# A hybrid attention layer on one core: the first two left factors of the last products loaded once, under the scans

## The chip, the cores and the metric

The kernel runs on one core of one Trainium2 chip. The metric is the time of one execution on the device in microseconds (us). Five engines work in parallel, each through its own list of instructions in order: TensorE (PE; its weight loads are listed as PEld), VectorE (DVE), ScalarE (ACT), GpSimd (POOL) and SyncE (SP). SP and POOL also start the transfers (DMA) between the core's memory and the device's main memory.

## The reference

One encoder layer on 1024 tokens of width 1024, with 16 learned meta tokens in front of them. `_gla_chunked` and `_neighbourhood_attention` stand in the reference above this part.

```python
h = concatenate([meta_tokens, x])
u = _rmsnorm(h, norm_g)
z = u @ w_in
gq, gk, gv, r_f, r_b, g_gate, nq, nk, nv, n_gate = split(z)
q, k, v = gq * GLA_DK ** -0.5, gk, gv                      # 4 heads of 128 keys, 256 values
lg_f = log_sigmoid(r_f @ w_decay_fwd + b_decay_fwd) / 16   # rank 16
lg_b = log_sigmoid(r_b @ w_decay_bwd + b_decay_bwd) / 16
o_f = _gla_chunked(q, k, v, lg_f)                          # a scan over chunks, one per direction
o_b = flip(_gla_chunked(flip(q), flip(k), flip(v), flip(lg_b)))
o_gla = _rmsnorm(o_f + o_b, gla_out_norm_g) * silu(g_gate)
qn, kn = _rmsnorm(nq, q_norm_g), _rmsnorm(nk, k_norm_g)    # 16 heads of 64
o_na = _neighbourhood_attention(qn, kn, nv, rpb, meta_bias) * silu(n_gate)
out = (h + concatenate([o_gla, o_na]) @ w_out)[16:]
```

The last line's product has an inner dimension of 2048: 1024 of `o_gla` and 1024 of `o_na`.

## The kernel before, in words

**Numbers in two parts.** A float32 factor is split into a high part (ScalarE copies it into a shorter format: `wh`, `uh`, `oh`, `lf[0]`, `kn[0]`) and a low part (VectorE subtracts the high part from the number: `wl`, `ul`, `ol`, `lf[1]`, `kn[1]`). `mm3` (L409) makes one product from three matmuls: high by high (L411), high by low (L412) and low by high (L413).

**Stages.** First the neighbourhood attention, eight pairs of heads `p`, with the input projection's matmuls as filler between its small matmuls. Then the gated linear attention of four heads `h` (`gla`, L1030): decays, a backward scan of seven steps (n = 7 to 1), a forward scan of eight (n = 0 to 7), again with projections as filler. Filler of the last head is the first part of the output projection: the rows of `w_out` for `o_na`, 16 steps `j` of two halves `f` (`out_proj`). At its end come the last products (`out_last`).

**The last products.** The rows of `w_out` that belong to `o_gla` make a product of two by two blocks, which is computed with seven block products in place of eight. `m` = 0 to 6 counts them, n = 0 to 3 the 128 columns within one, so there are 28 steps `j` = 4m + n of 12 matmuls. Their left factors are, in order, quadrant 11, quadrant 12, the sums s1, s4, s2, s3 and quadrant 22; `R` holds the quadrants (512 x 512, in four pieces of 256 KB) and the sums. Their right factors are blocks of `w_out` and the sums T and U, which accumulating transfers on POOL's queue build (L1426) and which are split like weights. `X` and `Y` are accumulators in TensorE's output memory; V takes -X after product 0.

**What sets the order.** `Sched` plans on a clock of its own, in TensorE's nanoseconds. `("gap", ns)` puts filler in for that long; `defer(ns, fn)` issues an operation when the clock has come that far; `PK_NS` is the gap ahead of a head's backward scan, `WD_NS` and `WD_LOW_NS` are deferrals of the decays' weights. What is fixed there is the order of each engine's list; on the chip each instruction waits for what it needs, and everything behind it on its engine waits too.

**Lines that the prediction names.** `wd_prep` (L1009) clears (POOL, L1012), copies (ScalarE, L1013) and completes (VectorE, L1016 and L1017) the decays' weights, at p = 2 for one direction and p = 4 for the other. L753 is VectorE's first step of a softmax, L772 and L774 its normalization, L792 VectorE's copy of transposed probabilities `PT`, L805 the matmuls that gather values with them. In a scan, L1161 transposes a chunk `pk` of the keys `ga` (made at L1107), L1163 and L1164 make its two parts `kn`, and `pu` are the matmuls on them; `at` and `ah` (L1244 to L1248) are VectorE's mask and parts of the chunk's scores, read by `po`. L262 and L263 make `wh` and `wl` of a projection's weight, L257 and L258 those of `w_out`, T and U. L1291 loads halves of 128 columns for the output projection (`oin`), L1308 and L1309 split them (`oh`), L1341 accumulates a half's result (`pout`) into `acc`. L1366 loads a piece of a quadrant (`r`), L1375 makes a sum's piece (`rs`, or into `r`), L1385 and L1389 split a left factor (`lf`), L1424 loads U, L1430 copies -X to V.

Buffers that matter: `oh` has three, `lf` five, weights nine (`NW`), each given back when TensorE has read it for the last time. The pool `op` is there from the last head on, the pool `tp` (quadrants, U) from the end of the scans on, in memory that the scans had.

Of the kernel before, what the change touches and what calls it, by code (L numbers as in the profile page):

```python
# [8 lines left out]
F32 = mybir.dt.float32  # L9
# [3 lines left out]
OP = mybir.AluOpType  # L13
# [24 lines left out]
PV_AT = (0.5, 0.5, 0.5, 0.6, 0.5, 0.5, 0.5, 0.5)  # L38
STEP_AT = (0.78, 2.0, 3.0, 4.0, 4.92, 6.0, 7.08, 8.0)
BWD_NS = (1800.0, 1523.0, 1844.0, 1892.0)  # L40
PK_NS = (3500.0, 2300.0, 2300.0, 2300.0)
AT_NS = 1085.0
R_NS = 2800.0
R0_NS = 1200.0
# [14 lines left out]
SILU_STEP = 1  # L59

WD_AT = (2, 4)
WD_NS = 20000.0
WD_LOW_NS = 5000.0

class Sched:

# [75 lines left out]
def kernel(  # L142
# [866 lines left out]
    def wd_prep(d):  # L1009

        st, w = G["wst"], G["wd"][d]
        pool.memset(f32(w[96:128]), 0.0)  # L1012
        act.activation(w[0:98], st[0:98], AF.Copy)  # L1013

        def low():
            dve.tensor_tensor(w[64:96], st[64:96], f32(w[64:96]), OP.subtract)  # L1016
            dve.scalar_tensor_tensor(w[96:98], f32(w[96:98]), ident[96:98, 97:98], st[96:98], OP.mult, OP.subtract)  # L1017

        S.defer(WD_LOW_NS, low)

    def decay_static():

# [251 lines left out]


    acc, oh, ol, op = {}, {}, {}, []
    steps = [(g, n) for g in (2, 3) for n in range(8)] + [(g, n) for g in (0, 1) for n in range(4)]
    R = {}

    def out_proj():  # L1280

        ld = {}

        def load(j):
            if j < len(steps):
# [12 lines left out]

        def halves(j):
            if j < len(steps):  # L1300
                g, n = steps[j]
                t = ld.pop(j)
                if j == 0:
                    o = shr.tile([128, 2, 4, 128], F32R, tag="zt", name=f"oh{g}_{n}", bufs=3)
                else:
                    o = op[0].tile([128, 2, 4, 128], F32R, tag="oh", name=f"oh{g}_{n}", bufs=3)
                oh[j], ol[j] = o[:, 0], o[:, 1]
                act.activation(oh[j], t, AF.Copy)  # L1308
                dve.tensor_tensor(ol[j], t, f32(oh[j]), OP.subtract)  # L1309

        def ahead(j):
            halves(j + 1)
            load(j + 3)

        for j in range(2):
            load(j)
        x_in(0)
        yield from dense_gg(3, lambda: halves(0))
        upool_cm.__exit__(None, None, None)
        op.append(ostack.enter_context(tc.tile_pool(name="op", bufs=1, side="right")))  # L1320
        load(2)
        for j in range(1, 4):
            x_in(j)
        for j, (g, n) in enumerate(steps[:16]):
            ahead(j)
            x_in(j + 4)
            if j == 9:
                wsum["T"] = op[0].tile([128, 4, 512], F32, name="T")
                sp.dma_start(wsum["T"], w_block(0, 0))
            if j == 11:  # L1330
                pool.dma_start(wsum["T"], w_block(0, 1), accum_op=OP.add)
            for f in range(2):
                ps = ps_tile("pd", f"pout{g}_{n}_{f}", 2)
                for k in range(4):
                    wh, wl = weights(("o", g), 4 * f + k)
                    mm3(ps, oh[j][:, k], ol[j][:, k], wh, wl, k == 0, k == 3)
                    if n == 7:
                        release()
                    yield 648
                a = acc[n][:, f * 512 : f * 512 + 512]  # L1340
                dve.tensor_tensor(a, a, ps, OP.add)  # L1341

        yield from out_last(ahead)

    def weights(key, i):
        while (key, i) not in split:
# [5 lines left out]

    def out_tiles(tp):

        for q in (22, 21, 11, 12, "s1", "s2"):
            R[q] = tp.tile([128, 4, 512], F32, name=f"r{q}")
        wsum["U"] = tp.tile([128, 4, 512], F32, name="U")
        op.append(tp)

    def rv(q, n):  # L1360
        return R[q][:, :, 128 * n : 128 * n + 128]
# [3 lines left out]
        ts = slice(512 * h + 128 * n, 512 * h + 128 * n + 128)  # L1365
        sp.dma_start(rv(q, n), o_scr[4 * g : 4 * g + 4, :, ts].rearrange("f p t -> p f t"))  # L1366

    def out_last(ahead):


        sums = {"s1": ("s1", 21, 22), "s2": ("s2", 11, "s1"), "s4": (12, 12, "s2"), "s3": (21, 21, 11)}
# [1 line left out]
        def add(s, n):  # L1373
            d, a, b = (rv(q, n) for q in sums[s])
            dve.tensor_tensor(d, a, b, OP.subtract)  # L1375

        left = (11, 12, "s1", 12, "s2", 21, 22)
        opnd = {}

        def operand(m, n):  # L1380

            t = rv(left[m], n)
            o = op[1].tile([128, 2, 4, 128], F32R, tag="lf", name=f"lf{m}_{n}", bufs=5)
            sign = -1.0 if m == 6 else 1.0
            act.activation(o[:, 0], t, AF.Copy, scale=sign)  # L1385
            if m == 6:
                dve.scalar_tensor_tensor(o[:, 1], t, -1.0, f32(o[:, 0]), OP.mult, OP.subtract)
            else:
                dve.tensor_tensor(o[:, 1], t, f32(o[:, 0]), OP.subtract)  # L1389
            opnd[m, n] = o  # L1390

        V = [op[0].tile([128, 512], F32, name=f"V{n}") for n in range(4)]

        def quad(q, n):
            return acc[n + 4 * (q // 10 - 1)][:, 512 * (q % 10 - 1) : 512 * (q % 10)]
# [13 lines left out]

        todo = {j: [] for j in range(28)}  # L1410
        for n in range(4):
            for q, j in ((22, (3, 3, 4, 4)), (21, (3, 3, 4, 4)), (11, (5, 5, 6, 6)), (12, (7, 7, 8, 8))):
                todo[j[n]].append(lambda q=q, n=n: quadrant_in(q, n))
            todo[5 + n].append(lambda n=n: add("s1", n))
            todo[7 + n].append(lambda n=n: add("s2", n))
            todo[9 + n].append(lambda n=n: add("s4", n))
            todo[15 + n].append(lambda n=n: add("s3", n))
            for m in range(2, 7):
                todo[4 * m + n - 2].append(lambda m=m, n=n: operand(m, n))
            todo[13 + n].append(lambda n=n: plus(11, n, X[n], store=True))  # L1420
            todo[18 + n].append(lambda n=n: [pool.dma_start(quad(q, n), V[n], accum_op=OP.add) for q in (12, 22)])
            todo[21 + n].append(lambda n=n: plus(21, n, V[n], OP.subtract))
            todo[21 + n].append(lambda n=n: put(12, n))
        todo[8].append(lambda: sp.dma_start(wsum["U"], w_block(1, 1)))  # L1424
        for j, (t, g, f) in {8: ("T", 1, 1), 10: ("U", 0, 1), 16: ("T", 1, 0)}.items():
            todo[j].insert(0, lambda t=t, g=g, f=f: pool.dma_start(wsum[t], w_block(g, f), accum_op=OP.add))  # L1426

        def result(m, n):
            if m == 0:
                act.activation(V[n], X[n], AF.Copy, scale=-1.0)  # L1430
            elif m == 2:
                plus(22, n, Y[n])
            elif m == 3:
                plus(12, n, Y[n])
# [6 lines left out]

        for j in range(28):
            m, n = divmod(j, 4)
            if j < 8:
                ahead(16 + j)
            for fn in todo[j]:
                fn()
            P = X if m in (0, 1, 4) else Y
# [3 lines left out]
            first = m in (0, 2, 4, 5)  # L1452
            for k in range(4):
                wh, wl = weights(("m", m), k)
                a, b = (oh[16 + j], ol[16 + j]) if m < 2 else (opnd[m, n][:, 0], opnd[m, n][:, 1])
                mm3(P[n], a[:, k], b[:, k], wh, wl, first and k == 0, k == 3, not first)
                if n == 3:
                    release(1000.0 * k)
                yield 648
# [147 lines left out]
```

## Time and profile before

| | us |
|---|---|
| median of three runs | 1122.23 |
| lowest and highest | 1119.29, 1124.56 |
| profiled execution, its own time | 1118.37 |
| its span | 1116.6 |
| TensorE busy | 1099.4 (98%) |
| VectorE busy | 750.4 (67%) |
| ScalarE busy | 564.5 (51%) |
| GpSimd busy | 220.7 (20%) |

The span is the profiled execution's from its first to its last instruction; its own time has 1.8 us more. The attention takes the span to about 600 us, the four heads' scans from there to about 1032, the last products from about 1028 to the end. The granted clock of TensorE was full in all but the last stretch. Rows of the timeline give start, duration and idle time of the engine before the row with what ended it; "x6" merges neighbours, and the end of a matmul is modelled, so matmuls overlap in the rows.

### The profile page before, as it was taken

What the parts mean: (1) busy time and instruction counts of PE and PEld (TensorE: products, weight loads), DVE (VectorE), ACT (ScalarE), POOL (GpSimd) and SP (SyncE); (2) the same over time, 40 slices, a digit from 0 to 9 for tenths busy, and PEclk for the clock granted to TensorE, in tenths of its full rate; (3) what the DMA queues carried; (4) which work ended last, traced back from release to release, by engine and by line L of the source; (5) the groups of instructions that cost most, each with busy time, mean ns of one, the idle gap of its engine ahead of it and who ended that gap; (6) DMA issues with size and microseconds to landing.
All of it is one profiled execution on the core that took longest, in us unless ns stands there. A gap on an engine that the chain in (4) does not pass through costs nothing.

```text
span 1116.6 us, 18945 instructions
## 1 busy us (share of the span) xinstructions
PE 1099.4 (98%) x6691; PEld 970.7 (87%) x6691; DVE 750.4 (67%) x1854; ACT 564.5 (51%) x1464; POOL 220.7 (20%) x442
## 2 busy tenths in 40 slices
PE   8999999999999999999999999999999999999998
PEld 7899898989989899898898789889889977887776
DVE  4666666776666767666764975776596578656485
ACT  6756475674656657565555441642443254313431
POOL 2733232332323233231100001000101000010011
PEclk9999999999999999999999999999999999999999
DMA  8720302112021210302124412503612365352967
GB/s 277 234 59 20 104 10 84 56 39 86 9 84 56 75 58 2 121 12 60 60 58 123 143 49 75 160 25 82 179 38 72 91 205 177 104 133 85 269 137 184
DMA packets 83591, 108.67 MB, mean 97 GB/s; under 512 B 6884, under 2 KB 51300, under 8 KB 83496
## 3 DMA queue, kind: packets, MB, share of 16 engines
q1 hardware_dynamic: 74344, 91.85, 26.5%
q0 software_dynamic: 8864, 15.47, 6.5%
q8 instruction: 53, 0.87, 0.3%
q14 instruction: 42, 0.34, 0.1%
q10 hardware_dynamic: 288, 0.14, 0.0%
HBM read 80.10 MB, written 21.04 MB: 91 GB/s over the span
## 4 chain that ended last, share of the span: by engine, by line
PE 83%; DVE 6%; ACT 3%; DMA 3%; SPq 2%; issue 1%; POOL 1%; DVEq 0%; POOLq 0%; ACTq 0%
PE pn_na L411 7%; PE pn_na L413 6%; PE pn_na L412 6%; PE po L805 4%; PE pp L786 3%; PE pn_gv L411 3%; PE pn_gv L413 3%; PE pn_gv L412 3%; PE pz_gz L411 3%; PE pz_na L413 3%; PE pz_na L412 3%; PE pz_na L411 3%; PE pz_gg L411 3%; PE pz_gz L412 3%; PE pz_gz L413 3%; PE pz_gg L412 3%
## 5 line engine op out<-in xcount | busy, mean ns | idle before, releaser
L411 PE MATMUL pn_na<-wh,uh 128*128 128x384 f32 x512 | 177.9, 347 | 2.0 <-ACT uh L362 1.2
L412 PE MATMUL pn_na<-wl,uh 128*128 128x384 f32 x512 | 172.7, 337 | 0.4 <-DVE wl L263 0.4
L413 PE MATMUL pn_na<-wh,ul 128*128 128x384 f32 x512 | 172.5, 337 | 0.2
L263 DVE SCALAR_TENSOR_TENSOR wl<-raw,gT,wh 128x256 fp32r<-128x256 f32 (+4 forms) x168 | 89.9, 574 | 37.6 <-ACT wh L262 36.7
L411 PEld LDWEIGHTS pn_na<-wh,uh 128*128 128x128 f32 x512 | 96.2, 188 | 8.0 <-issue 4.6
L262 ACT ACTIVATE wh<-raw,gT 128x256 fp32r<-128x256 f32 (+4 forms) x168 | 88.1, 576 | 21.9 <-PE pz_gz L412 14.0
L758 ACT ACTIVATE P<-P,sm 128x384 f32<-128x384 f32 x96 | 58.5, 609 | 77.9 <-DVE sm L753 77.2
L412 PEld LDWEIGHTS pn_na<-wl,uh 128*128 128x128 f32 x512 | 96.4, 188 | 1.7 <-DVE wl L263 1.3
L413 PEld LDWEIGHTS pn_na<-wh,ul 128*128 128x128 f32 x512 | 96.2, 188 | 0.9 <-DVE ul L364 0.9
L213 POOL TENSOR_SCALAR post<-post 128x1 f32<-128x1 f32 x32 | 6.9, 215 | 375.8 <-ACT on L1212 375.8
L214 POOL TENSOR_TENSOR ss<-ss,epsm 128x4 f32<-128x4 f32 x64 | 74.5, 1163 | 5.3
L411 PE MATMUL pn_gv<-wh,uh 128*128 128x256 f32 (+1 forms) x256 | 75.3, 294 | 0.0
L413 PE MATMUL pn_gv<-wh,ul 128*128 128x256 f32 (+1 forms) x256 | 72.8, 284 | 0.0
L412 PE MATMUL pn_gv<-wl,uh 128*128 128x256 f32 (+1 forms) x256 | 72.7, 284 | 0.0
L753 DVE CUSTOM_DVE_ANT_0 P<-s,wt 128x416 f32<-128x416 f32 (+1 forms) x128 | 65.4, 547 | 1.0
L774 DVE TENSOR_SCALAR P<-P,sm 128x384 f32<-128x384 f32 (+1 forms) x128 | 58.3, 455 | 11.5 <-ACT P L758 0.5
L1212 ACT ACTIVATE on<-po 128x256 f32<-128x256 f32 x32 | 12.3, 383 | 89.6 <-PE po L413 89.4
L772 DVE RECIPROCAL sm<-sm 128x1 f32<-128x1 f32 x128 | 20.8, 162 | 53.3 <-POOL sm L760 49.0
L411 PE MATMUL pz_na<-uh,wh 128*128 128x512 f32 x128 | 53.2, 416 | 0.0
L411 PE MATMUL pout<-wh,oh 128*128 128x512 f32 x128 | 52.3, 409 | 0.2 <-DVE acc L1341 0.2
L411 PE MATMUL pz_gz<-uh,wh 128*128 128x512 f32 x128 | 52.5, 410 | 0.0
L786 PE MATMUL pp<-ident,P 128*128 128x128 f32 (+1 forms) x384 | 52.5, 272 | 0.0
(378 smaller groups left out, 3030.1 us busy)
## 6 DMA issues: line engine op xcount, KB each, us to landing
raw<-in_w_na_dram SPq DMA_DIRECT2D x56, 256.0 KB, 3.4
v_scr<-gvst SPq DMA_DIRECT2D x64, 128.0 KB, 2.3
raw<-in_w_o_dram SPq DMA_DIRECT2D x28, 256.0 KB, 3.2
v<-v_scr POOLq DMA_DIRECT2D x4, 1536.0 KB, 9.1
oin<-o_scr SPq DMA_DIRECT2D x24, 256.0 KB, 3.3
VM<-vnat SPq DMA_DIRECT2D x8, 512.0 KB, 3.5
o_scr<-ng SPq DMA_DIRECT2D x8, 512.0 KB, 2.6
raw<-in_w_gz_dram SPq DMA_DIRECT2D x16, 256.0 KB, 2.7
```

The source lines that it names most:

```text
L214: pool.tensor_tensor(dst, dst, epsm[: dst.shape[0], :eng_n], OP.pow)
L262: act.activation(wh[:, ts], r[:, ts], AF.Copy, scale=g)
L263: dve.scalar_tensor_tensor(wl[:, ts], r[:, ts], g, f32(wh[:, ts]), OP.mult, OP.subtract)
L411: pe.matmul(ps, ah, bh, start=start, stop=False, skip_group_check=more)
L412: pe.matmul(ps, ah, bl, start=False, stop=False, skip_group_check=more)
L413: pe.matmul(ps, al, bh, start=False, stop=stop, skip_group_check=more)
L753: dve.tensor_tensor_reduce(P[:, :n], ps[:, :n], wt[2 * p + a][:, off : off + n], -1.0, 3.0e38, OP.add, OP.min, mx)
L758: act.activation(loc, loc, AF.Exp, scale=-1.0, bias=mx, accum_out=sm[:, a : a + 1])
L772: dve.reciprocal(r, s)
L774: dve.tensor_scalar(loc, loc, r, None, OP.mult)
L786: pe.transpose(pp[:w, c * 128 : c * 128 + 128], Ps[a][0][:, c0 : c0 + w], ident)
L805: pe.matmul(po[0][64 * a : 64 * a + 64, u4 * 128 : u4 * 128 + 128], V[:, 64 * a : 64 * a + 64], PT[a][:w, c * 128 : c * 128 + 128], start= ...
```

## The change

It has five parts. (1) Quadrants 11 and 12 are loaded once, in pieces, during steps 12 to 15 of the output projection, which run under the last head's scans; they are the left factors of products 0 and 1 and the quadrants of the later sums. Before, products 0 and 1 loaded the same numbers as eight more halves `oin`, and the quadrants were loaded after the scans. (2) The left factors of all products are split by `operand`, two steps ahead; the first two are split within the output projection's last two steps. The sums come one step earlier, and the accumulating transfers stand last in their steps and not first. (3) The copy of -X to V is issued at the start of steps 3 and 4 and not after each step of product 0, and V lies in the pool `tp`. (4) The decays' weights are cleared and copied earlier, and their two low parts are issued apart. (5) The gap ahead of the first head's backward scan is shorter, and the halves of step 1 of the output projection are split after the first half of step 0.

```diff
-PK_NS = (3500.0, 2300.0, 2300.0, 2300.0)
+PK_NS = (2900.0, 2300.0, 2300.0, 2300.0)
...
-WD_NS = 20000.0
-WD_LOW_NS = 5000.0
+WD_NS = 11000.0
+WD_LOW_NS = (7900.0, 20100.0)
...
         def low():
             dve.tensor_tensor(w[64:96], st[64:96], f32(w[64:96]), OP.subtract)
+
+        def low_bias():
             dve.scalar_tensor_tensor(w[96:98], f32(w[96:98]), ident[96:98, 97:98], st[96:98], OP.mult, OP.subtract)
 
-        S.defer(WD_LOW_NS, low)
+        S.defer(WD_LOW_NS[0], low)
+        S.defer(WD_LOW_NS[1], low_bias)
...
-    steps = [(g, n) for g in (2, 3) for n in range(8)] + [(g, n) for g in (0, 1) for n in range(4)]
+    steps = [(g, n) for g in (2, 3) for n in range(8)]
...
-        for j, (g, n) in enumerate(steps[:16]):
-            ahead(j)
+        for j, (g, n) in enumerate(steps):
+            if j:
+                halves(j + 1)
+            load(j + 3)
             x_in(j + 4)
...
             for f in range(2):
+                if (j, f) == (0, 1):
+                    halves(1)
...
+            if j == 10:
+                for q in (11, 12):
+                    R[q] = op[0].tile([128, 4, 512], F32, name=f"r{q}")
+            if j > 11:
+                quadrant_in(11, j - 12)
+                quadrant_in(12, j - 12)
+            if j > 13:
+                operand(0, j - 14)
+        yield from out_last()
...
-        for q in (22, 21, 11, 12, "s1", "s2"):
+        for q in (22, 21, "s1", "s2"):
             R[q] = tp.tile([128, 4, 512], F32, name=f"r{q}")
         wsum["U"] = tp.tile([128, 4, 512], F32, name="U")
         op.append(tp)
+        V.extend(tp.tile([128, 512], F32, name=f"V{n}") for n in range(4))
...
+    def operand(m, n):
+
+        t = rv(left[m], n)
+        if m < 2:
+            o = op[0].tile([128, 2, 4, 128], F32R, tag="oh", name=f"lf{m}_{n}", bufs=3)
+        else:
+            o = op[1].tile([128, 2, 4, 128], F32R, tag="lf", name=f"lf{m}_{n}", bufs=5)
...
-            for q, j in ((22, (3, 3, 4, 4)), (21, (3, 3, 4, 4)), (11, (5, 5, 6, 6)), (12, (7, 7, 8, 8))):
-                todo[j[n]].append(lambda q=q, n=n: quadrant_in(q, n))
-            todo[5 + n].append(lambda n=n: add("s1", n))
-            todo[7 + n].append(lambda n=n: add("s2", n))
-            todo[9 + n].append(lambda n=n: add("s4", n))
+            for q in (22, 21):
+                todo[(3, 3, 4, 4)[n]].append(lambda q=q, n=n: quadrant_in(q, n))
+            todo[3 if n < 3 else 4].append(lambda n=n: act.activation(V[n], X[n], AF.Copy, scale=-1.0))
+            todo[4 + n].append(lambda n=n: add("s1", n))
+            todo[6 + n].append(lambda n=n: add("s2", n))
+            todo[8 + n].append(lambda n=n: add("s4", n))
             todo[15 + n].append(lambda n=n: add("s3", n))
-            for m in range(2, 7):
-                todo[4 * m + n - 2].append(lambda m=m, n=n: operand(m, n))
+            for m in range(7):
+                if 4 * m + n > 1:
+                    todo[4 * m + n - 2].append(lambda m=m, n=n: operand(m, n))
...
-            todo[j].insert(0, lambda t=t, g=g, f=f: pool.dma_start(wsum[t], w_block(g, f), accum_op=OP.add))
+            todo[j].append(lambda t=t, g=g, f=f: pool.dma_start(wsum[t], w_block(g, f), accum_op=OP.add))
...
-            if m == 0:
-                act.activation(V[n], X[n], AF.Copy, scale=-1.0)
-            elif m == 2:
+            if m == 2:
                 plus(22, n, Y[n])
```

TensorE has the same instructions as before; their order differs only in the first head's scans. How the instructions stand on three lists shows what moves.

**VectorE, the decays' weights at p = 4** (`P`, `sm`: two softmaxes, four steps apart in `s`; `wd`: the weights). Before:

```order
L753 ISA P_4426,sm_4414<-s_4423,wt_3900 128x416
L753 ISA sm_4414 128x1
L1016 TENSOR_TENSOR wd_142<-wdst_4068,wd_142 32x512
L1017 SCALAR_TENSOR_TENSOR wd_142<-wd_142,ident,wdst_4068 2x512
L772 RECIPROCAL sm_4414<-sm_4414 128x1
L774 TENSOR_SCALAR P_4418<-P_4418,sm_4414 128x3x128
```

And now:

```order
L753 ISA P_4347,sm_4335<-s_4344,wt_3900 128x416
L753 ISA sm_4335 128x1
L1016 TENSOR_TENSOR wd_142<-wdst_4068,wd_142 32x512
L772 RECIPROCAL sm_4335<-sm_4335 128x1
L774 TENSOR_SCALAR P_4339<-P_4339,sm_4335 128x3x128
```

The first low part stands one softmax step earlier, and the second 29 rows behind it, ahead of a reciprocal one softmax step later than before. On ScalarE the copy (L1013) stands two steps earlier than before, behind the gate's first exponential.

**VectorE, the first head's second forward step** (`gt`: the gate; `wl`: a weight's low part; `at`, `ah`: the scores and their parts). Before:

```order
L1216 SCALAR_TENSOR_TENSOR on_7816<-po_7792,post_7815,gn 128x256
L617 TENSOR_TENSOR gt_7351<-gt_7351,gq_6516 128x512
L263 SCALAR_TENSOR_TENSOR wl_7846<-raw_7455,gT,wh_7845 128x256 x2
L617 TENSOR_TENSOR gt_7351<-gt_7351,gq_6516 128x512
L617 TENSOR_TENSOR gt_7351<-gt_7351,gk_6517 128x512 x2
L1226 TENSOR_TENSOR og_7859<-po00t,gt_7351 128x256
L1244 TENSOR_TENSOR at_7865<-pa_7862,tri 128x128
L1245 COPY_PREDICATED at_7865<-tri,pa_7862 128x128
L1247 CAST ah_7868<-at_7865 128x128
```

And now:

```order
L617 TENSOR_TENSOR gt_7351<-gt_7351,gq_6516 128x512 x2
L617 TENSOR_TENSOR gt_7351<-gt_7351,gk_6517 128x512 x2
L1229 TENSOR_TENSOR og_7848<-po00t,gt_7351 128x256
L1247 TENSOR_TENSOR at_7854<-pa_7851,tri 128x128
L1248 COPY_PREDICATED at_7854<-tri,pa_7851 128x128
L1250 CAST ah_7857<-at_7854 128x128
L1251 TENSOR_TENSOR ah_7857<-at_7854,ah_7857 128x128
L1262 TENSOR_TENSOR tf_7867<-pu_7863,sf_7790 128x256
L1264 TENSOR_SCALAR sf_7869<-tf_7867,c_7641 128x256
L263 SCALAR_TENSOR_TENSOR wl_7875<-raw_7455,gT,wh_7874 128x256 x2
```

The weight's low part stood among the gate's products, ahead of `at` and `ah`; now it follows them.

**SP's queue, the last loads** (`r22` to `r12`: pieces of quadrants). Before:

```order
L1366 DMA r22_11868<-o_scr_74 128x4x128
L1366 DMA r21_11869<-o_scr_74 128x4x128
L1366 DMA r11_11870<-o_scr_74 128x4x128 x4
L1366 DMA r12_11871<-o_scr_74 128x4x128 x4
L1424 DMA U_11874<-in_w_o_dram 128x4x512
L1405 DMA out_0_dram<-acc0_10518 128x512
```

And now:

```order
L1378 DMA r22_11863<-o_scr_74 128x4x128
L1378 DMA r21_11864<-o_scr_74 128x4x128
L1439 DMA U_11867<-in_w_o_dram 128x4x512
L1418 DMA out_0_dram<-acc0_10518 128x512
L1418 DMA out_0_dram<-acc1_10756 128x512
```

Eight loads between the last of quadrants 22 and 21 and the load of U are gone from there; they stand ahead of and between the last two stores of the scans' results. The four last loads of halves (L1291), three of which stood ahead of the first piece of quadrant 22, are gone.

More of the change, by code (lines that the diff above doesn't have):

```diff
@@ L1309, in halves @@
                 dve.tensor_tensor(ol[j], t, f32(oh[j]), OP.subtract)
-        def ahead(j):
-            halves(j + 1)
-            load(j + 3)
         for j in range(2):
@@ L1341, in out_proj @@
                 dve.tensor_tensor(a, a, ps, OP.add)
-        yield from out_last(ahead)
+            if j == 10:
[7 more added lines that the diff above has]
+        yield from out_last()
     def weights(key, i):
@@ L1366, in quadrant_in, with out_last @@
         sp.dma_start(rv(q, n), o_scr[4 * g : 4 * g + 4, :, ts].rearrange("f p t -> p f t"))
-    def out_last(ahead):
+    left = (11, 12, "s1", 12, "s2", 21, 22)
+    opnd, V = {}, []
+    def operand(m, n):
[4 more added lines that the diff above has]
+            o = op[1].tile([128, 2, 4, 128], F32R, tag="lf", name=f"lf{m}_{n}", bufs=5)
+        sign = -1.0 if m == 6 else 1.0
+        act.activation(o[:, 0], t, AF.Copy, scale=sign)
+        if m == 6:
+            dve.scalar_tensor_tensor(o[:, 1], t, -1.0, f32(o[:, 0]), OP.mult, OP.subtract)
+        else:
+            dve.tensor_tensor(o[:, 1], t, f32(o[:, 0]), OP.subtract)
+        opnd[m, n] = o
+    def out_last():
         sums = {"s1": ("s1", 21, 22), "s2": ("s2", 11, "s1"), "s4": (12, 12, "s2"), "s3": (21, 21, 11)}
@@ L1375, in add @@
             dve.tensor_tensor(d, a, b, OP.subtract)
[L1377 to L1392, printed above, removed]
         def quad(q, n):
@@ L1443, in out_last @@
             m, n = divmod(j, 4)
-            if j < 8:
-                ahead(16 + j)
             for fn in todo[j]:
@@ L1454, in out_last @@
                 wh, wl = weights(("m", m), k)
-                a, b = (oh[16 + j], ol[16 + j]) if m < 2 else (opnd[m, n][:, 0], opnd[m, n][:, 1])
-                mm3(P[n], a[:, k], b[:, k], wh, wl, first and k == 0, k == 3, not first)
+                o = opnd[m, n]
+                mm3(P[n], o[:, 0, k], o[:, 1, k], wh, wl, first and k == 0, k == 3, not first)
                 if n == 3:
```

## The prediction

> **What bounds the kernel now.** I read the page's busy shares first, then TensorE's waits, then the timeline at each wait, then the other engines there.
>
> ```profile
> PE 1099.4 (98%) x6691; PEld 970.7 (87%) x6691; DVE 750.4 (67%) x1854; ACT 564.5 (51%) x1464; POOL 220.7 (20%) x442
> PE pm L413 <- DVE lf L1389: 4.2, 3, 1.8
> ```
>
> TensorE bounds the kernel, and the change removes none of its instructions. So a gain can come only from its idle time, 1116.6 - 1099.4 = 17.2 us, and only from idle time at places that the edits touch. The second row names the largest wait. The timeline of TensorE shows where the touched waits lie (start, duration, instruction, idle time before it and who ended it):
>
> ```profile
> 232.95 0.54 PE L805 MATMUL po<-PT,vnat 128*64 128x128 f32 x5 [0.98 <-DVE PT L792]
> 368.03 0.54 PE L805 MATMUL po<-PT,vnat 128*64 128x128 f32 x5 [0.97 <-DVE PT L792]
> 629.28 0.39 PE L413 MATMUL pu<-v,kn 128*128 128x256 f32 x1 [0.27 <-DVE kn L1164]
> 657.78 0.39 PE L411 MATMUL po<-vx,ah 128*128 128x256 f32 x1 [0.94 <-DVE ah L1247]
> 917.16 0.39 PE L411 MATMUL pu<-v,kn 128*128 128x256 f32 x1 [0.39 <-ACT kn L1163]
> 917.93 0.39 PE L413 MATMUL pu<-v,kn 128*128 128x256 f32 x1 [0.26 <-DVE kn L1164]
> 921.75 0.50 PE L411 MATMUL pout<-wh,oh 128*128 128x512 f32 x1 [0.20 <-DVE acc L1341]
> 1053.96 0.40 PE L411 MATMUL pm<-wh,lf 128*128 128x512 f32 x1
> 1054.20 0.40 PE L412 MATMUL pm<-wl,lf 128*128 128x512 f32 x1
> 1056.37 0.50 PE L413 MATMUL pm<-wh,lf 128*128 128x512 f32 x1 [1.77 <-DVE lf L1389]
> 1063.59 0.50 PE L413 MATMUL pm<-wh,lf 128*128 128x512 f32 x1 [1.15 <-DVE lf L1389]
> 1076.73 0.50 PE L413 MATMUL pm<-wh,lf 128*128 128x512 f32 x1 [1.28 <-DVE lf L1389]
> ```
>
> Two such matmuls in a row start 0.24 us apart (1053.96 to 1054.20); over the wait at 1056.37 the starts are 2.17 apart, so it costs 1.93, which is its idle time plus 0.16 for the refill. I add 0.16 to each wait. A step of the last products is 12 matmuls, about 2.8 us.
>
> **The change part by part. The decays' weights.** The chain of waits (start, duration, instruction) runs through their preparation at the second direction:
>
> ```profile
> 357.22 0.53 POOL wd L1012
> 357.78 0.63 ACT wd L1013
> 362.67 0.68 DVE wd L1016
> 363.38 0.75 DVE wd L1017
> 367.42 0.57 DVE PT L792
> 356.24 0.17 DVE L772 RECIPROCAL sm<-sm 128x1 f32<-128x1 f32 x1 [1.04 <-POOL sm L760]
> 370.16 0.17 DVE L772 RECIPROCAL sm<-sm 128x1 f32<-128x1 f32 x1 [1.04 <-POOL sm L760]
> ```
>
> All four pieces, 2.59 us, stand ahead of the copy PT at 367.42, for which TensorE waits until 368.03. The first direction has the same wait 135 us earlier, at 232.95. The changed order puts the copy and the clearing some 12 us earlier, the first low part right ahead of the reciprocal at 356.24, whose 1.04 us of idle time it fits (0.68), and the other behind the wait, near the reciprocal at 370.16 with the same idle time (0.75). The wait of 1.13 (0.97 + 0.16) is less than the 2.59 taken away, so both go: 0.98 + 0.97 + 0.32 = 2.3 us. Of the copy's new place the trace shows only neighbours: it delays the softmax behind it by at most its own 0.63, and that is still less than 2.59 - 1.13 = 1.46. Bounds: 0 (it meets another wait) to 2.3. I take 2.3.
>
> **The shorter gap of the first head.** TensorE meets every step of that head's scans one piece of filler work (three matmuls, 0.70 us) earlier. At the wait of 657.78 VectorE stood behind a weight's low part:
>
> ```profile
> 653.91 0.88 DVE L263 SCALAR_TENSOR_TENSOR wl<-raw,gT,wh 128x256 fp32r<-128x256 f32 x2 [1.38 <-ACT wh L262]
> 624.49 1.22 DVE L1107 SCALAR_TENSOR_TENSOR ga<-ga,gk 128x1024 f32<-128x1024 f32 x1
> 626.30 0.27 PE L1161 MATMUL pk<-ident,ga 128*128 128x128 f32 x1
> ```
>
> In the changed order that low part comes after `ah`, so VectorE neither idles 1.38 nor works 0.88 ahead of it, 2.26 in all. TensorE comes 0.70 earlier and the wait was 1.10, together 1.80; it goes. Against that, the first transpose moves from 626.30 to 625.60, and what it reads is ready at 624.49 + 1.22 = 625.71: a new wait of 0.11 and a refill, about 0.25. The wait at 629.28 stays, since transpose and factor move together. Sum: 1.10 - 0.25, rounded to 0.9 less. Bounds: 1.5 less (both waits go, 1.10 + 0.43) to 0.3 more (the old ones stay and the new one comes).
>
> **The halves of the second step** (after the first half of the first step, not before):
>
> ```profile
> 916.32 0.63 ACT L1308 ACTIVATE oh<-oin 128x512 fp32r<-128x512 f32 x1 [2.09 <-DVE gt L483]
> 916.85 0.43 ACT L1163 ACTIVATE kn<-pk 128x128 fp32r<-128x128 f32 x2
> 916.98 0.69 DVE L1309 TENSOR_TENSOR oh<-oin,oh 128x512 fp32r<-128x512 f32 x1
> 918.84 2.29 DVE L1081 TENSOR_TENSOR_SCAN ga<-hm,gm 128x1024 f32<-128x1024 f32 x1
> ```
>
> ScalarE held two factors `kn` back behind `oh`, and VectorE another 0.6. Without both, the wait of 917.16 goes (0.55) and that of 917.93 halves (0.42 to about 0.2). The wait of 921.75 stays: the scan of 2.29 ahead of its accumulation shifts with TensorE. The moved low part now follows that accumulation and is ready about when it is first read. Sum: 0.75 less, bounds 0 to 1.3.
>
> **The last products.** The loads on SP's queue, the accumulating ones on POOL's, and who waits for them:
>
> ```profile
> 1037.04 2.09 SPq L1366 DMA_DIRECT2D r<-o_scr  x4
> 1040.68 15.93 SPq L1366 DMA_DIRECT2D r<-o_scr  x12
> 1056.65 0.69 SPq L1424 DMA_DIRECT2D U<-in_w_o_dram  x1
> 1063.68 1.28 POOL L1426 DMA_DIRECT2D U<-in_w_o_dram  x1 [19.31 <-DMA U<-in_w_o_dram]
> 1055.02 0.69 DVE L1375 TENSOR_TENSOR rs<-r,rs 128x512 f32<-128x512 f32 x1 [6.40 <-DMA r<-o_scr]
> 1073.52 0.63 ACT L257 ACTIVATE wh<-U 128x512 fp32r<-128x512 f32 x1 [4.53 <-DMA U<-in_w_o_dram]
> 1056.65 6.20 DMA U<-in_w_o_dram
> 1063.68 9.76 DMA U<-in_w_o_dram
> 1040.13 0.60 ACT L1430 ACTIVATE V<-pm 128x512 f32<-128x512 f32 x1 [0.65 <-PE pm L413]
> 1055.00:1060.00 5.00, 3.63 (x15) 2.73 (x16) 4.98 (x9) 1.72 (x4) 0.00 (x0) 1.00 1.14 336
> ```
>
> Two causes make all three waits. At 1055.02 VectorE has idled 6.40 us for the first piece of quadrant 11, and works without a gap from there (4.98 of 5 us), so the waits of 1056.37 and 1063.59 are its arrears. At 1073.52 ScalarE waits for U, which SP issued at 1056.65, behind twelve loads, and whose accumulation took 9.76. In the changed order quadrants 11 and 12 lie loaded before the scans end, eight of the twelve loads ahead of U are gone and so are four loads of halves: U is issued at about 1041, after the remaining eight at 0.7 each. It lands by about 1047, at the 6.20 of its load today, its accumulation by about 1058, 15 us before 1073. VectorE's 6.40 us of idling vanish, more than the arrears of 1.93 + 1.31. Sum: 1.77 + 1.15 + 1.28 + 0.48 = 4.7 less. Bounds: 1.0 (see the first rival) to 5.0.
>
> At nothing stand the new eight loads under the scans (eight loads of halves of the same 256 KB go; none is read within 8 us), the sums one step earlier (VectorE idle as above), and the four copies to V. These are ScalarE's, 0.6 each, now one at a time ahead of the step that reuses their bank; the first is due when step 4 begins, at 1040.1 by the last of today's copies, which follows step 3. Without that cover they cost 0.6 each, 2.4.
>
> The sum: 2.3 + 0.9 + 0.75 + 4.7 = 8.65, say 8.7 us. The profiled execution took 1118.37 (span 1116.6 and 1.8 around it), so it would take 1109.7. The three runs shown have a median of 1122.23, 3.9 above it; against that, 1113.5, which I predict.
>
> **The rivals. A: T or the queue takes the place of U.** In the changed order VectorE can split the fourth product's second weight only when step 7 gives its buffer back, near 1040.1 + 4 x 2.8 = 1051.3; four operations of 0.6 later, at about 1053.5, stands the first weight from T, and everything behind it waits.
>
> ```profile
> T<-in_w_o_dram POOLq DMA_DIRECT2D x1, 1024.0 KB, 11.0
> ```
>
> T was issued at 1043.04 and landed at 1054.0. U's 1.05 MB now run beside it; at the 336 GB/s of the window above that is 3.1 us. If in place of the eight loads gone (2.1 MB, 6.2 us) T lands 6.2 later, at 1060.2, the operand of step 11 (due at 1040.1 + 7 x 2.8 = 1059.7) is ready five VectorE operations later, at 1063.2: 3.5 lost, gain 5.2, 1117.0. Against it: fewer bytes are asked for from 1035 on, not more. [...]
>
> **B: the decays' wait is only moved.** The softmax behind the new copy runs late by 0.63 and some gather waits instead. For it: the chain of waits runs there without a gap. Against: 1.46 us of slack. Gain 8.7 - 2.3 = 6.4: 1115.8.
>
> **C: the copies to V come late**, since V now lies in memory that is free only when the scans' last transfers are done; the change then doesn't hide what it says. If free only at 1040.68, the first copy ends 1.2 after 1040.1 and the other three cost 0.6 each, 3.0: gain 5.7, 1116.5. Against: the first load into that memory was issued at 1037.04.
>
> **D: slower.** TensorE meets VectorE 0.70 us earlier at all 15 scan steps of the first head. If each of seven backward steps pays 0.43 (as at 629.28) and each of eight forward ones 0.43 + 1.10, that is 15.3, 13.8 over today's; minus 7.75 elsewhere it is 6 slower, 1128.2. It decides from 0.52 us a step. Against: one forward wait and one backward wait is all the head has now.
>
> **How the numbers follow.** Forecast 0.65, A 0.12, B 0.10, C 0.08, D 0.05. The forecast's own range is 1110 (10.1 off, the largest of the bounds, halfway between the two levels) to 1117 (5.2 off the median). The range 1108 to 1119 goes down to all waits gone at the profiled execution's level (1118.4 - 10.1) and up past A, B and C; D is left out. A measurement of this kernel tells about 0.5%, 5.6 us, from no change: faster is 0.62 of the forecast, 0.03 of A, 0.08 of B, 0.02 of C, 0.75; slower 0.04 of D; the rest, 0.21, is the same.
>
> **What would show it.** TensorE's waits on `PT` near 232 and 367 gone, and low parts of `wd` in idle time of VectorE; no wait on `ah` near 657, a short one on `ga` near 626; one wait on `kn` left near 917; U issued near 1041 and no idle time of VectorE for `r`. It is wrong if `pm` still waits by more than 1 us, or if new waits on `kn` or `ah` stand in the first head.

## The result, and the profile after

| | before | after |
|---|---|---|
| median of six runs each, us | 1119.49 | 1110.79 |
| lowest and highest | 1117.73, 1124.56 | 1110.35, 1112.25 |
| profiled execution, its own time | 1118.37 | 1110.68 |
| its span | 1116.6 | 1108.9 |

The ratio is 0.9922 (95% interval 0.9907 to 0.9938), 8.7 us faster. The prediction had named a gain of 8.7 and a time of 1113.5; the six runs of the kernel before lie lower than the three that it started from. The sum came out right, but one of its four terms did not come at all, and what filled its place was in no term: that both gains read 8.7 is in part luck.

The page's busy shares after the change:

```profile
PE 1098.5 (99%) x6691; PEld 971.1 (88%) x6691; DVE 751.3 (68%) x1854; ACT 564.6 (51%) x1464; POOL 220.9 (20%) x442
```

TensorE has as good as the same work (1099.4 us before) in a span that is 7.7 shorter. Four rows of its list of waits (in total, times, longest, us):

```profile
PE po L805 <- DVE PT L792: 1.9, 5, 0.5
PE pn_na L411 <- ACT uh L362: 0.8, 1, 0.8
PE po L411 <- DVE ah L1250: 0.4, 1, 0.4
PE pout L411 <- DVE acc L1344: 0.3, 1, 0.3
```

`pm`, 4.2 us before, is gone from the list. `PT` was 2.1 in three waits and is 1.9 in five. (Lines behind the edits have moved by a few numbers: L1250 is L1247 of before, L1344 is L1341.) The timeline of TensorE at the places that the prediction named:

```profile
231.89 0.54 PE L805 MATMUL po<-PT,vnat 128*64 128x128 f32 x5 [0.37 <-DVE PT L792]
244.46 0.54 PE L805 MATMUL po<-PT,vnat 128*64 128x128 f32 x5 [0.50 <-DVE PT L792]
367.23 0.54 PE L805 MATMUL po<-PT,vnat 128*64 128x128 f32 x5 [0.37 <-DVE PT L792]
379.79 0.54 PE L805 MATMUL po<-PT,vnat 128*64 128x128 f32 x5 [0.50 <-DVE PT L792]
625.45 0.40 PE L413 MATMUL pz_gg<-uh,wl 128*128 128x512 f32 x1
625.99 0.30 PE L1164 MATMUL pk<-ident,ga 128*128 128x128 f32 x1
915.48 0.28 PE L412 MATMUL pu<-v,kn 128*128 128x256 f32 x1
915.89 0.39 PE L413 MATMUL pu<-v,kn 128*128 128x256 f32 x1
919.80 0.47 PE L411 MATMUL pout<-wh,oh 128*128 128x512 f32 x1 [0.28 <-DVE acc L1344]
```

By the prediction's own measure, idle time plus the 0.16 that it read from the matmuls' starts around 1056.37, the terms came out so:

| term | before | after | gain | predicted |
|---|---|---|---|---|
| decays' weights | 2.27 | 4 waits, 1.74 + 0.64 = 2.38 | -0.1 | 2.3 |
| first head | 1.53 | 0.30 (625.45 to 625.99, less 0.24) | 1.2 | 0.9 |
| halves of step 1 | 1.33 | 0.29 (915.48 to 915.89, less the 0.12 of 918.41 to 918.53) + 0.44 = 0.73 | 0.6 | 0.75 |
| last products | 4.68 | 0 | 4.7 | 4.7 |

That is 6.4 of the 7.7 us between the two profiled executions. 0.4 more is the wait on `uh` at the kernel's start (1.2 before, 0.8 after), which no edit touches; it was between 0.8 and 2.6 in the profiles taken for this work. The rest is not assigned to a place.

In the last products, the timeline of SP's queue, of GpSimd, and of ScalarE at T and U:

```profile
1039.20 1.56 SPq L1439 DMA_DIRECT2D U<-in_w_o_dram  x1
1048.29 1.28 POOL L1441 DMA_DIRECT2D U<-in_w_o_dram  x1 [6.05 <-PE pm L413]
1052.75 0.63 ACT L257 ACTIVATE wh<-T 128x512 fp32r<-128x512 f32 x1 [3.14 <-DMA T<-in_w_o_dram]
1060.69 0.62 ACT L257 ACTIVATE wh<-U 128x512 fp32r<-128x512 f32 x1
```

And the two transfers into U, with the time from issue to landing at the end of the row:

```profile
U<-in_w_o_dram SPq DMA_DIRECT2D x1, 1024.0 KB, 8.1
U<-in_w_o_dram POOLq DMA_DIRECT2D x1, 1024.0 KB, 9.4
```

U is issued at 1039.20 (before: 1056.65), and its accumulated part lands at 1048.3 + 9.4 = 1057.7, ahead of its reader at 1060.69. ScalarE still waits 3.14 us for T, but nothing of it reaches TensorE. The window in which TensorE had been busy for 3.63 of 5 us (the columns, as in the prediction's row: the window and its length; busy time and instructions of TensorE, its weight loads, VectorE, ScalarE and GpSimd; granted clock; share of the DMA engines; GB/s):

```profile
1055.00:1060.00 5.00, 5.00 (x23) 4.07 (x22) 5.00 (x9) 2.16 (x4) 0.00 (x0) 1.00 0.35 65
```

It is now busy for all 5, and so is VectorE.

### The profile page after: what moved, and what is told of

Same layout as the page of the kernel before. It is cut to its first block, busy times and chain, and to the rows that moved or that the text cites. A ratio compares the mean times of both kernels' runs of the same rounds, so it can differ in the third digit from the quotient of the medians.

```text
span 1108.9 us, 18934 instructions
## 1 busy us (share of the span) xinstructions
PE 1098.5 (99%) x6691; PEld 971.1 (88%) x6691; DVE 751.3 (68%) x1854; ACT 564.6 (51%) x1464; POOL 220.9 (20%) x442
## 4 chain that ended last, share of the span: by engine, by line
PE 84%; DVE 5%; ACT 5%; POOL 2%; DMA 2%; issue 1%; SPq 0%; DVEq 0%; ACTq 0%; POOLq 0%
PE pn_na L411 6%; PE pn_na L412 5%; PE pn_na L413 5%; PE po L805 4%; PE pn_gv L411 3%; PE pp L786 3%; PE pn_gv L412 3%; PE pn_gv L413 3%; PE pz_gz L411 3%; PE pz_gg L411 3%; PE pz_na L413 3%; PE pz_na L412 3%; PE pz_na L411 3%; PE pz_gz L412 3%; PE pz_gz L413 3%; PE pz_gg L412 3%
```

## The experiments

**Putting the two halves of the change apart.** First, everything but the last products, which are as before:

```diff
-PK_NS = (3500.0, 2300.0, 2300.0, 2300.0)
+PK_NS = (2900.0, 2300.0, 2300.0, 2300.0)
-WD_NS = 20000.0
-WD_LOW_NS = 5000.0
+WD_NS = 11000.0
+WD_LOW_NS = (7900.0, 20100.0)
...
-            ahead(j)
+            if j:
+                halves(j + 1)
+            load(j + 3)
...
+                if (j, f) == (0, 1):
+                    halves(1)
```

> The changed kernel with the last products as before: halves loaded for products 0 and 1, quadrants loaded after the scans, V copied after each step of product 0; decays' weights, first gap and halves of step 1 as changed. By the prediction's terms: 3.95 us faster than before, 1115.5. By the waits read after the change (decays nothing, gap 1.2, halves 0.7): 1.7 faster, 1117.8 at a level of 1119.5; waits on PT as in the changed kernel, the three waits on lf back with 4.2 us in all.

Measured: a ratio of 0.9985 (0.9972 to 0.9998), 1.7 us faster (0.2 to 3.1), medians 1120.39 and 1117.92. It is the sum read from the waits, and the prediction's 3.95 lies outside the interval. Of the three waits on `lf` that were expected back, its profile has two, of 1.90 and 1.28; the granted clock was 0.50 behind both, for 3.4 us from about 1055.0 and from about 1075.5, of which more below. The other way round, the kernel before with the new last products alone (the change's diff without its first three hunks, without `if j:` and without the two lines on `halves(1)`):

> The kernel before with the new last products alone (loads, operands, sums, V). Theory: its three waits on lf and the half second lost at the end go, 5.0 us faster than before, 1114.5; the waits near 233 and 368 (0.98, 0.97), 629, 657 and 917 are those of the kernel before. Rival (the parts help each other, so that the last products gain less alone): a wait on lf or on T's or U's parts of 0.5 or more, under 4 us faster.

Measured: 0.9945 (0.9925 to 0.9966), 6.2 us faster (3.8 to 8.4). No wait on `lf` is left, and the waits that the small edits are to remove are there as before; three of them:

```profile
234.12 0.54 PE L805 MATMUL po<-PT,vnat 128*64 128x128 f32 x5 [0.97 <-DVE PT L792]
630.43 0.39 PE L413 MATMUL pu<-v,kn 128*128 128x256 f32 x1 [0.27 <-DVE kn L1164]
658.98 0.39 PE L411 MATMUL po<-vx,ah 128*128 128x256 f32 x1 [0.94 <-DVE ah L1247]
```

As far as their intervals tell, the two parts add up: 1.7 + 6.2 = 7.9, where both together gave 8.7 with an interval of 6.9 to 10.4. So the last products made most of the gain. The small edits made 1.7 of the predicted 3.95, and at most 3.1 by their interval.

**Two causes in the last products, or one.** The prediction put two of the three waits down to VectorE's arrears after quadrant 11, and the third to the place of U on SP's queue. One line of the kernel before tells them apart:

```diff
-        todo[8].append(lambda: sp.dma_start(wsum["U"], w_block(1, 1)))
+        todo[6].append(lambda: sp.dma_start(wsum["U"], w_block(1, 1)))
```

> The kernel before with one edit: U's load stands on SP's queue ahead of the four loads of quadrant 12, and not behind them; nothing else. Theory (two causes): the wait near 1076.7 (1.28), which the place of U in the queue made, goes, and the arrears of quadrant 11 near 1056.4 and 1063.6 (1.77 and 1.15) stay: 1.4 us faster, 1118.1. Rival (one cause: the queue and the memory are simply full): U lands no earlier by more than 2 us, or quadrant 12 becomes late and a new wait on lf of 1 us or more stands near 1063 or 1080; no gain.

Measured: 0.9966 (0.9955 to 0.9978), 3.8 us faster, more than the 1.4 expected, and there was one wait on `lf` in TensorE's timeline where two were to stay:

```profile
1057.95 0.50 PE L413 MATMUL pm<-wh,lf 128*128 128x512 f32 x1 [2.25 <-DVE lf L1389]
```

In this profile the granted clock (the third number from the end of a window's row) was halved behind that wait, from 1059.1 on for 3.4 us:

```profile
1059.00:1060.00 1.00, 1.00 (x4) 0.80 (x3) 1.00 (x3) 1.00 (x3) 0.00 (x0) 0.56 1.06 410
1060.00:1061.00 1.00, 1.00 (x3) 0.71 (x3) 1.00 (x3) 0.19 (x1) 0.00 (x0) 0.50 1.08 361
```

With TensorE at a clock of 0.50, VectorE could catch up in these 3.4 us, and then a second wait would not show. Hence a second profile of the same kernel:

> The same kernel as e3_u_ahead, looked at once more, because its profile showed the clock halved behind the first wait on lf, which hides what VectorE's arrears cost at full clock. Theory (arrears of quadrant 11 stay): where the clock stays full behind the first wait (about 2 us, near 1056), a second wait on lf of about 1.2 stands near 1063; where it halves, there is none. Rival (the earlier U also ends the second wait): the clock stays full and no second wait on lf over 0.3 stands there.

Its timeline, of TensorE and of SP's queue:

```profile
1057.11 0.50 PE L413 MATMUL pm<-wh,lf 128*128 128x512 f32 x1 [1.75 <-DVE lf L1389]
1064.33 0.50 PE L413 MATMUL pm<-wh,lf 128*128 128x512 f32 x1 [1.15 <-DVE lf L1389]
1052.18 2.90 SPq L1424 DMA_DIRECT2D U<-in_w_o_dram  x1
```

This time the clock stayed full (1.00 from 1052 to 1080), and both arrears stand there, 1.75 and 1.15 as in the kernel before (1.77 and 1.15). The third wait is gone with U issued 4.5 us earlier. So there are two causes, as predicted: the place of U's load makes the third wait and not the first two. That the late quadrant 11 makes those is read from VectorE's 6.40 us of idle time for it (the prediction's row at 1055.02); no run moved that quadrant alone. The 2.4 us beyond the expected 1.4 are not in the waits; what the clock may have to do with them comes below.

**Why the decays' weights gained nothing.** After the change, the timeline of ScalarE and VectorE around the second direction's preparation:

```profile
344.68 0.63 ACT L1013 ACTIVATE wd<-wdst 98x512 fp32r<-98x512 f32 x1
345.22 0.46 ACT L512 ACTIVATE sq<-pn_na,rs 128x256 f32<-128x256 f32 x1
355.55 0.68 DVE L1016 TENSOR_TENSOR wd<-wdst,wd 32x512 fp32r<-32x512 f32 x1
356.56 0.16 DVE L772 RECIPROCAL sm<-sm 128x1 f32<-128x1 f32 x1 [0.33 <-POOL sm L760]
369.42 0.16 DVE L772 RECIPROCAL sm<-sm 128x1 f32<-128x1 f32 x1 [1.10 <-POOL sm L760]
370.53 0.75 DVE L1019 SCALAR_TENSOR_TENSOR wd<-wd,ident,wdst 2x512 fp32r<-2x512 f32 x1
371.31 0.16 DVE L772 RECIPROCAL sm<-sm 128x1 f32<-128x1 f32 x1
```

The first low part (355.55) did go into idle time, as predicted: 0.33 of it is left behind. The bias's low part (370.53) did not. The idle time of 1.10 lies ahead of the first reciprocal of that softmax, and this piece was put behind it, ahead of the second, which had none in the kernel before either (371.33). And the copy at 344.68 has work without a gap behind it on ScalarE. The clearing, which moved with the copy, holds nothing else up; GpSimd's timeline:

```profile
344.13 0.52 POOL L1012 MEMSET wd<- 32x512 f32 x1
346.30 0.19 POOL L213 TENSOR_SCALAR ss<-ss 128x4 f32<-128x4 f32 x1 [1.65 <-DVE ss L517]
```

Two suspects, then, and for each its own waits: the copy for those near 232 and 367, the bias's part for those near 244 and 380. One constant moves the bias's part alone:

```diff
-WD_LOW_NS = (7900.0, 20100.0)
+WD_LOW_NS = (7900.0, 18500.0)
```

> The changed kernel, with only the low part of the bias (L1019, 0.75 us) moved: it stands ahead of the first reciprocal of its softmax and no longer ahead of the second. Theory (its place): the changed kernel idles 1.10 us ahead of that first reciprocal (369.42) and not at all ahead of the second, so there the 0.75 is covered. TensorE's waits on PT near 244.4 and 379.8 (0.50 each) go, those near 231.9 and 367.2 (0.37 each) stay; 1.5 us less idle time in all, with the refills. Rival (load): VectorE's chain from softmax to softmax has no slack anywhere, so the two low parts cost their 1.43 us wherever they stand; the waits near 244 and 380 stay at 0.3 or more, or as much wait appears at another PT of the same pair of heads.

Measured: the waits near 244 and 380 are gone; 233.69 (0.36) and 368.28 (0.37) stay. Its one time, 1111.53, doesn't show the gain: in this execution the wait on `uh` at the kernel's start was 2.51 in place of 0.80. The copy alone:

```diff
-WD_NS = 11000.0
-WD_LOW_NS = (7900.0, 20100.0)
+WD_NS = 8300.0
+WD_LOW_NS = (10600.0, 23300.0)
```

> The changed kernel, with only ScalarE's copy and the clearing of the decays' weights moved some 4 us earlier, to where ScalarE idles 1.44 us ahead of a softmax (341.62); both low parts stay where the change put them. Theory (its place): the copy of 0.63 at 344.68 delays the squares and the meta tokens' kvt behind it, and this delay runs down VectorE's chain to PT; so the waits near 231.9 and 367.2 (0.37 each) go, those near 244.4 and 379.8 (0.50 each) stay; 1.3 us less idle time. Rival (the low part at 355.55 is the cause): the waits near 231.9 and 367.2 stay at 0.3 or more.

Measured: the opposite. The waits near 234 and 370 more than doubled, and the time was 1113.89. The timeline of ScalarE, VectorE and TensorE there:

```profile
344.75 0.63 ACT L1013 ACTIVATE wd<-wdst 98x512 fp32r<-98x512 f32 x1 [2.69 <-POOL wd L1012]
346.79 0.16 DVE L772 RECIPROCAL sm<-sm 128x1 f32<-128x1 f32 x1 [2.86 <-POOL sm L760]
370.36 0.54 PE L805 MATMUL po<-PT,vnat 128*64 128x128 f32 x5 [0.80 <-DVE PT L792]
```

The copy overwrites part of what GpSimd clears, so it waits for the clearing, which had moved with it and stood behind other work of GpSimd; ScalarE waited 2.69 us, and a softmax with it. So this run does not tell what the copy alone does. With the same two constants, and the clearing at the start of the pair of heads:

```diff
         G["wst"] = st
+        pool.memset(f32(G["wd"][d][96:128]), 0.0)
...
         st, w = G["wst"], G["wd"][d]
-        pool.memset(f32(w[96:128]), 0.0)
```

> The changed kernel, with ScalarE's copy of the decays' weights where the last try had it (1.44 us of idle time ahead of a softmax), and with the clearing on GpSimd put at the start of the pair of heads, so that the copy waits for nothing; both low parts stay where the change put them. Theory (the copy's place): without 0.63 ahead of the squares and kvt, the waits on PT near 231.9 and 367.2 (0.37 each) go or fall under 0.2, those near 244.4 and 379.8 (0.50 each) stay. Rival (the low part ahead of the reciprocal of 356.56 is the cause of 0.37): the waits near 231.9 and 367.2 stay at 0.3 or more.

What is left of the waits on `PT` in TensorE's timeline, beside one of 0.18 near 515:

```profile
245.29 0.54 PE L805 MATMUL po<-PT,vnat 128*64 128x128 f32 x5 [0.49 <-DVE PT L792]
380.12 0.54 PE L805 MATMUL po<-PT,vnat 128*64 128x128 f32 x5 [0.49 <-DVE PT L792]
```

The waits near 232 and 367 are gone. Here too the one time, 1111.06, doesn't show it: the wait on `uh` was 1.92, and behind it the clock was 0.50 for 3.4 us from 27.8 on. So each suspect made its own pair of waits: the copy the first, the bias's low part the second. Both put right:

```diff
-WD_NS = 11000.0
-WD_LOW_NS = (7900.0, 20100.0)
+WD_NS = 24600.0
+WD_LOW_NS = (400.0, 6400.0)
```

> The changed kernel, with all pieces of the decays' weights in idle time of their engines: the copy behind ScalarE's copy of PT at 358.1 (2.96 us idle behind it), the low part ahead of the first reciprocal of the next softmax (362.99, 0.97 idle ahead of it), the bias's low part ahead of the first reciprocal of the one behind (369.42, 1.10 idle). Theory (place): all four waits on PT near 232, 244, 367 and 380 go; 2.8 us less than the changed kernel's 1110.8, so 1108.0, a ratio to the kernel before of 0.9897. Rival (load): 1.43 us of VectorE's work stay on the path of each direction; at least two waits of 0.3 to 1 stay, and the time is 1110 to 1111.

VectorE's timeline, with idle time left ahead of both reciprocals:

```profile
360.53 0.68 DVE L1016 TENSOR_TENSOR wd<-wdst,wd 32x512 fp32r<-32x512 f32 x1
361.68 0.16 DVE L772 RECIPROCAL sm<-sm 128x1 f32<-128x1 f32 x1 [0.46 <-POOL sm L760]
366.97 0.75 DVE L1019 SCALAR_TENSOR_TENSOR wd<-wd,ident,wdst 2x512 fp32r<-2x512 f32 x1
367.98 0.17 DVE L772 RECIPROCAL sm<-sm 128x1 f32<-128x1 f32 x1 [0.26 <-POOL sm L760]
```

And the row of `PT` among TensorE's waits:

```profile
PE po L805 <- DVE PT L792: 0.2, 1, 0.2
```

All four waits are gone (the 0.2 left is at 512 us; the kernel before has it too). The span is 1106.6, 2.3 less than after the change, as the 2.38 of the table want it. The time is 1108.95, with a ratio to the kernel before of 0.9899 (0.9883 to 0.9916): the fastest kernel of this study. The expected 1108.0 was 1 us too good. That VectorE had no slack at all for these pieces, the rival, has fallen.

**The first head at a still shorter gap.**

```diff
-PK_NS = (2900.0, 2300.0, 2300.0, 2300.0)
+PK_NS = (2300.0, 2300.0, 2300.0, 2300.0)
```

> The changed kernel with the gap ahead of the first head's backward scan shorter by another piece of filler (2300 and not 2900), so TensorE meets each step of that head's scans another 0.70 us earlier. Theory: what the first transpose reads is done at a time that VectorE sets, so its wait near 625.5 grows from 0.31 to about 1.0, and behind it transposes and factors move together; no step pays on top, and the end moves by less than 0.5 us. Rival (the prediction's slower case): the steps of the scans have no room left, 0.43 or more at each of the seven backward ones, 3 us or more in new waits on kn and ah between 625 and 680.

TensorE's timeline at the first transpose:

```profile
625.16 0.40 PE L413 MATMUL pz_gg<-uh,wl 128*128 128x512 f32 x1
626.41 0.30 PE L1164 MATMUL pk<-ident,ga 128*128 128x128 f32 x1 [0.85 <-ACT wh L262]
```

From 625.16 to 626.41 are 1.25, less 0.24: the first transpose waits 1.01 us in place of 0.30, 0.70 more for 0.70 earlier. (The row names a copy of ScalarE's; VectorE's `ga`, which the transpose reads, ended in that profile at 624.99 + 1.22 = 626.21.) Up to 690 us no step of that head's scans waits. So the first transpose takes up whatever TensorE comes too early, and the steps behind it move along. Its single time, 1112.24, is 1.56 above the changed kernel's profiled execution. At the kernel's start its wait on `uh` is 0.87 longer (1.67), and that on `wh` 0.30 longer (1.20). What is left, about 0.4, is within the 0.5 that was expected, but one execution can't tell it from 0.

## Why the prediction was right, and where it was wrong

- **The last products (4.7 predicted, 4.7 in the waits).** Each step held: U issued at 1039.20 (predicted 1041), landed and accumulated by 1057.7 (1058), VectorE without idle time for `r`, no wait on `pm`. Only the margin was smaller than said: ScalarE reads U from 1060.69 on, 3 us after it has landed and not 15.
- **The first head (0.9 predicted, 1.2).** The step that failed is "the wait at 629.28 stays, since transpose and factor move together". It went with the wait at 657.78. The new wait of 0.30 on `ga` came where and as it was worked out (0.25).
- **The halves (0.75 predicted, 0.6).** The wait at 917.16 went, that at 917.93 fell from 0.42 to 0.29 where 0.2 was said, and that at 921.75 grew from 0.36 to 0.44.
- **The decays' weights (2.3 predicted, -0.1).** Two steps failed. The passage "the other behind the wait, near the reciprocal at 370.16 with the same idle time" took the idle time of a softmax's first reciprocal for that of its second; in VectorE's list it stood between the two, so it could only fill idle time ahead of the second. And "it delays the softmax behind it by at most its own 0.63, and that is still less than 2.59 - 1.13 = 1.46" set the copy's delay against work taken from a later place: the delay of 0.63 on a chain without gaps reached the next `PT` whatever was saved elsewhere. This is rival B, which had a chance of 0.10, and its gain of 6.4 is what the waits make; but of the four waits only two come from the copy that it spoke of.
- **The other rivals.** A: T did hold ScalarE for 3.14 us, but landed at about 1052.7, not later than before (1054.0): issued 2.1 earlier, it took 11.8 beside U in place of 11.0. C: the copies to V ran from 1033.29 to 1039.2; ScalarE waited 0.18 for the scans' last store ahead of the first, and no matmul waits for one. D: the shorter gap costs nothing per step, even at twice the shortening.
- **The size of the whole.** Without the decays' term the sum is 6.4, and the profiled executions differ by 7.7. The medians differ by 8.7. So the match with the forecast's 8.7 is luck as far as 2.3 us of it go. Part of these may be the clock, which no term held: see the last section.

## What to carry to other kernels

In these runs a moved piece of work was covered only by the idle time right at its new place in the list (the bias's low part of 0.75 by the 1.10 ahead of the first reciprocal, and not at all ahead of the second), so read which of two like instructions it stands next to, and ask what the piece itself waits for (here a clearing on another engine that moved with it). Here a delay on a chain without gaps was not paid for by work removed further along it: behind the copy of 0.63 two waits of 0.37 stayed. And behind 16 of the 27 waits of TensorE of 1.28 us or more the granted clock was 0.50 for about 3.4 us, an estimated 1.7 us on top of the wait, so long waits go first.

## What the runs showed of the hardware

**The clock behind long waits.** Behind some waits the granted clock fell to 0.50 for 3.4 us, then came back to 1.00. In the kernel with the old last products, a wait in TensorE's timeline:

```profile
1054.31 0.50 PE L413 MATMUL pm<-wh,lf 128*128 128x512 f32 x1 [1.90 <-DVE lf L1396]
```

and the first of the four windows of 1 us with a lower clock behind it:

```profile
1055.00:1056.00 1.00, 1.00 (x4) 0.72 (x3) 1.00 (x3) 1.00 (x3) 0.00 (x0) 0.51 1.16 344
```

The other three have 0.50, 0.50 and 0.78, so the four together miss 1.71 us of full clock. At half the clock for 3.4 us TensorE loses an estimated 1.7 us, unless VectorE's arrears would have stopped it anyway. To see what decides, VectorE was given idle copies ahead of `PT` at sixteen places (the output stays the same), their number rising over the span in one kernel and falling in the other:

```diff
+                    for _ in range(p + 1 if u in (2, 5) else 0):
+                        dve.tensor_copy(Ps[a][0][:, 0:384], pp[:, 0:384])
                     dve.tensor_copy(t[:w, e0:e1], pp[:w, e0:e1])
```

> A measurement of what a wait of TensorE costs beside its own length. In profiles taken so far the granted clock fell to 0.50 for about 3.3 us behind 6 of 11 waits of 1.28 to 2.51 us, and behind none of some twenty waits up to 1.21. Here VectorE makes p + 1 idle copies of 0.55 us ahead of the copy of PT at the third and sixth block of rows of each pair of heads p = 0 to 7 (the output stays the same), so that TensorE meets waits of about 0 to 4 us at known places. Theory (the clock answers to idle time within a short stretch): no halving behind waits under 1.2, some behind 1.3 to 3, one behind every wait over 3.4; each 3.3 to 3.5 us long at 0.50, so some 1.7 us dearer than the wait. Rival (the clock falls for reasons of its own): halvings stand at places without waits, or as often behind short waits as behind long ones.

> The same with 8 - p idle copies, so that the long waits come early in the span and the short ones late. Theory: the halvings go with the length of the wait and not with the place: behind most waits over 2 us in the first pairs of heads, behind none under 1.2 in the last ones. Rival: they stand at the same places of the span as in the run before it.

Three waits of the rising kernel in TensorE's timeline:

```profile
249.31 0.54 PE L807 MATMUL po<-PT,vnat 128*64 128x128 f32 x5 [2.14 <-DVE PT L794]
319.86 0.54 PE L807 MATMUL po<-PT,vnat 128*64 128x128 f32 x5 [2.05 <-DVE PT L794]
543.33 0.90 PE L807 MATMUL po<-PT,vnat 128*64 128x128 f32 x5 [4.20 <-DVE PT L794]
```

Over 4 us from each of them (from 249, 320 and 543) the granted clock was 1.00, 0.57 and 0.50. The two kernels took 1148.69 and 1151.71 us.

Over all profiles of this study, after the first 7 us of the span:

| length of the wait, us | waits | clock halved behind it |
|---|---|---|
| 0.70 to 1.24 | 49 | 0 |
| 1.28 to 1.99 | 13 | 6 |
| 2.05 to 2.74 | 8 | 5 |
| 3.28 to 4.40 | 6 | 5 |

The halvings go with the length and not with the place: in the falling kernel they stand behind the waits of 4.40, 3.88, 3.92, 2.67 and 2.74 us between 119 and 417 us, and behind none of 1.51 (487.54) and 1.24 (556.14) later. So the theory held; of the six waits of 3.28 and more, only the one of 3.28, still under the theory's bound of 3.4, was followed by no halving.

Waits of one length (2.14 and 2.05) differ, and so do executions of one kernel. The traces show a pattern that goes with it. In the falling kernel the halvings begin at 27.54, 119.70, 194.80, 269.89, 344.98 and 416.66: these are 92.16, 75.10, 75.09, 75.09 and 71.68 us apart, or 27, 22, 22, 22 and 21 times 3.413. In the other three profiles with more than one halving they are whole multiples of it apart too: 6 with the old last products (1055.02 and 1075.50), 302 with U ahead (28.28 and 1059.12), 86, 22 and 43 in the rising kernel (26.72, 320.28, 395.38 and 542.15). Cut the span of each of the thirteen profiles into such stretches (where there is no other, a halving just behind the span gives the cuts: at 1116.69 in the kernel before, at 1110.36 in the changed one). Then TensorE's idle time within one stretch sorts the cases of these profiles: the clock was halved in the next stretch in 14 of 14 after 1.79 us or more, in 2 of 9 after 1.51 to 1.75, and in none of 141 after 0.25 to 1.44. Only the one halving of two stretches, behind the wait of 4.20, went on after a stretch with less, 1.18. The waits of 2.05 and 3.28 in the rising kernel, stretch by stretch:

```profile
316.87:320.28 3.41, 1.36 (x22) 1.12 (x21) 3.31 (x9) 0.02 (x1) 0.43 (x1) 1.00 0.51 154
320.28:323.69 3.41, 3.41 (x16) 3.08 (x11) 1.88 (x6) 2.94 (x7) 0.00 (x0) 0.50 0.00 0
463.64:467.05 3.41, 1.87 (x19) 1.38 (x18) 3.31 (x6) 0.75 (x2) 1.36 (x1) 1.00 0.48 151
467.05:470.46 3.41, 1.67 (x15) 1.50 (x16) 2.34 (x8) 1.27 (x5) 0.00 (x0) 1.00 0.01 3
```

The first lies whole in one stretch, 2.05 of 3.41 us idle, and the next has half the clock. The second is cut in two, 1.54 and 1.74 us, and no halving follows. This was read from the finished profiles; no run was made to test it.

**What it means for the times.** In 16 of 27 executions of the kernel before, the mean granted clock over the execution was under 1.000 (down to 0.995); their median is 1120.99, that of the other 11 is 1119.26, and that of all 1120.41. One halving takes 0.0015 from such a mean (half of 3.4 us in 1118). So in these executions the kernel before loses some 1.2 us in its median, an estimate from 1120.41 and 1119.26, to halvings that its profiled execution does not show. The changed kernel's median loses none: four of its six executions had full clock, and their median is the 1110.79 of all six. What this makes of the 8.7 is not shown. The executions of the kernel before behind that figure have no clock on record, and between executions of full clock the medians, 1119.26 and 1110.79, are still 8.5 apart. Of the 2.3 us that the four terms leave open, only the 0.4 of `uh` has a place, in the profiled executions. The kernel with U ahead has one long wait less; its 2.4 us beyond the expected gain may in part be the same, but its interval begins at 2.5 us, and this was not settled.
